# Two layers with expert blocks on one core: a bound on the experts' scatters, unmodulated rows, and one fp32 product in an output projection's last pass

## The chip, the core and the metric

The kernel runs on one core of a Trainium2 chip, in one launch. The metric is the device time in microseconds, from the start to the end of an execution. TensorE (PE in the profile) multiplies matrices and transposes, VectorE (DVE) and ScalarE (ACT) work element by element, GpSimd (POOL) does so too and issues the indirect transfers, and SyncE (SP) issues the plain ones. The granted clock of TensorE is given in the profile as a share of 2.4 GHz: 1.00 or 0.50 (1.2 GHz), and means of the two.

## The reference

T = 512 rows of width D = 1024 in fp32 go through two layers. Both have the same ending: a mixing part (attention and others) whose output is multiplied by `w_out` and added to x behind a gate, a norm, a modulation by the scale and shift of the layer's condition, and a mixture of experts on the modulated rows.

```python
mix = jnp.concatenate([attn, hg], axis=-1) @ w_out[l]
x = x + ga1 * rmsnorm(mix, ln1_post[l])
h = rmsnorm(x, ln2_pre[l]) * (1.0 + sc2) + sh2
y = hierarchical_moe(h, ...)          # layer 1: 32 experts, 2 per row
...
x = x + g_mix * (merged @ w_out)
h2 = modulate(rms_norm(x, norm_ffn_g), sh_ffn, sc_ffn).reshape(b * s, d)
y = moe_ffn(h2, ...)                  # layer 2: 64 experts, 8 per row, and a shared one
```

An expert multiplies its rows by gate and up weights (1024 x 256 each), takes silu(gate) * up, and multiplies by down weights (256 x 1024). The result, times the row's weight, is added to the row's sum over its experts. So layer 1 adds 512 x 2 = 1024 rows and layer 2 adds 512 x 8 = 4096.

## The kernel before

All instructions go through a recording helper, so each has line 131 in the profile; one has to go by the names of tiles. `whole` (line 1733) calls the stages: `dense1`, the experts of layer 1 (`e1.run`), `dense2` with `out2`, the experts of layer 2 (`e2.run`), and `last`. Within a stage, tasks are generators, and a scheduler (`Flow`, line 152) runs the one that is due first by a virtual clock, which books an estimated cost for every instruction (`Clock.note`). The order of instructions on each engine is fixed when the program is built; a change in the number of instructions may shift a few of them.

**Weights.** SP loads weights in chunks of 128 x 1024 fp32 (512 KB) into pools `w` and `wx`, in the order in which they are used, as buffers come free. In the dense stages a product of fp32 accuracy is made of three fp32r instructions (`mm3`): weights and activations are both split into `hi` (a rounded copy, by ScalarE in `split_hi`) and `lo` (the rest, by VectorE in `split_lo`). Chunks whose split isn't wanted have `raw` set; the experts multiply in plain fp32 from the raw chunk.

**Output projection of layer 1.** `dense1` runs `w_out` in two passes, p = 0 for row tiles 0 and 1, p = 1 for tiles 2 and 3 (a tile is 128 rows), each with its own eight chunks `q_["o", p]`. The activations of tile n are two halves of 128 x 512, which `mixed` (line 1036) splits. Each pass has 8 chunks x 2 tiles x 2 column halves = 32 products of 128 x 512.

**After the projection.** `Post.pair` (line 1814) takes the sums of two tiles: it adds x behind the gate, makes the norm (tiles `u`, in the code `ms`), and starts `Route.tile` (line 1903) on each. That one transposes the normed rows on TensorE, modulates the transposed copy while it leaves PSUM (VectorE and ScalarE, scale and shift per partition), and runs the router's products and the choice of experts, many small VectorE instructions. Once both tiles of the pair have been transposed (`seen`), `pair` lets GpSimd modulate the rows themselves, in place, and store them to `h2_d` (`ha_d` in layer 1, `hb_d` in layer 2). For this the gate, shift and scale are loaded as broadcast rows. `Route.choose` and `Route.finish` come after all four tiles; the experts' loads of weights wait for the numbers they give.

**Experts.** Each expert has blocks of a fixed number of slots, 16 to 128, written out in `PLAN1` (1440 slots in 32 blocks) and `PLAN2` (5296 slots in 71 blocks). `Experts.block` turns the router's result into a list of row numbers, one per slot. An empty slot p of a block gets T + p, from `beyond`. GpSimd gathers the rows of `h2_d` into `xg` by this list, with the bound T - 1, so numbers above it are skipped. `Experts.xT` (line 2244) transposes the block on TensorE, four pieces into each of two PSUM banks; ScalarE copies one bank into `xT`, VectorE the other, with one instruction each. Then come the products with gate and up weights, `a`, its transposes `aT`, the products with down weights, and `add` (line 2330): the result `y` goes to `acc_d` by an accumulating scatter of GpSimd, without a bound. `acc_d` has T + 128 rows, so that empty slots add to the last 128, which nobody reads. `zeros` clears it beforehand. The transposes of the next expert's blocks come in TensorE's order ahead of the second half of the current one's gate and up products (`run`, line 2373).

Of the kernel before, what the change touches and what calls it, by code (L numbers as in the profile page):

```python
# [12 lines left out]
BF16 = mybir.dt.bfloat16  # L13
# [3 lines left out]
ALU = mybir.AluOpType  # L17
# [4 lines left out]
P = 128  # L22
# [191 lines left out]
class Body:  # L214
# [182 lines left out]
    def steps(self, queued, n, jobs, evac, kd=KD, pre=None, early=None):  # L397
# [6 lines left out]
        def one(c, j, sel):  # L404
            ahead = None
            for i in sel:
                kind, c0, width, act, view = jobs[i]
                if outs[i] is None:
                    outs[i] = view(self.bank())
                for jj in range(c.kd):  # L410
                    s = slice(jj * n + c0, jj * n + c0 + width)
                    wt = (c.hl[0][:, s], c.hl[1][:, s])
                    ac = act(j + jj)
                    L, R = (wt, ac) if kind == "T" else (ac, wt)
                    self.mm3(outs[i], L, R, j + jj == 0, j + jj == kd - 1)
                    if jj < c.kd - 1:
                        yield
                if j + c.kd == kd:
                    evac(i, outs[i])
                if ahead:  # L420
                    self.split_lo(ahead)
                    ahead = None
                elif self.si < self.ci + self.ls and self.loaded(READY):
                    ahead = self.split_hi()
                yield
            self.split_lo(ahead)

# [103 lines left out]
    def ada_mask(self):  # L531

        nc = self.nc
        m = self.mask = self.c_const([P, 256])
# [34 lines left out]
    def ada_row(self, acc, b, part, dst, gain=None, plus=0.0, cols_=None):  # L569
# [11 lines left out]
        nc.sync.dma_start(cols(dst), r)  # L581
# [90 lines left out]
    def dense1(self, x1_d, h2_d, route, x1, acc1, acc2):  # L672
# [9 lines left out]
        for p in range(2):  # L682
            q_["o", p] = self.add_chunks(I["w_out"], D, KD)
        x1.queue(route)
# [28 lines left out]
        post = Post(self, True, mod[0:3], I["x"], x1_d, h2_d, route)  # L713
        route.mod = self.c_tile([P, 8]), self.c_tile([P, 8])
# [3 lines left out]
        def row(i):  # L718
            yield 8.0
            post.load(i, self.u)  # L720

        def ada(parts):
            for part in parts:
# [3 lines left out]
                if part < 5:  # L727
                    rows.append(fl.start(row(part - 2)))

        def zeros():  # L730
# [9 lines left out]
            for t in range(NT + 1):  # L740
                nc.sync.dma_start(acc1[t * P : (t + 1) * P], z)
                yield 5.0
            nc.sync.dma_start(acc2[T : T + P], z)
# [83 lines left out]
        for p in range(2):  # L827
            fl.until_(lambda: E.done[2 * p] and E.done[2 * p + 1] and E.att[2 * p] and E.att[2 * p + 1])
            jobs = []
            for t in (2 * p, 2 * p + 1):  # L830
                act = (lambda t: lambda j: tuple(x[:, j % 4 * P : j % 4 * P + P] for x in E.half[t][j // 4]))(t)
                jobs += [("tok", half * 512, 512, act, full) for half in range(2)]
# [203 lines left out]
    def mixed(self, E, n, half, x, done):  # L1036

        hl = self.h(F32R), self.h(F32R)
# [143 lines left out]
    def dense2(self, acc_d, x2_d, route):  # L1182
# [15 lines left out]
        route.mod = self.c_tile([P, 8]), self.c_tile([P, 8])  # L1198
# [255 lines left out]
    def out2(self, mg, t_mg, x2_d, x3_d, h2_d, route, acc_d, e2):  # L1454
# [4 lines left out]
        post = Post(self, False, m[2:5], x2_d, x3_d, h2_d, route)  # L1459
        for i in range(3):  # L1460
            post.load(i, self.r4)
# [271 lines left out]
    def whole(self):  # L1733
        nc, tc, I, fl = self.nc, self.tc, self.I, self.flow
        dr = lambda n, r=T: self.dr.tile([r, D], F32, name=n)
        x1, x2, x3, ha, hb, acc1, acc2 = dr("x1_d"), dr("x2_d"), dr("x3_d"), dr("ha_d"), dr("hb_d"), dr("acc1_d", T + P), dr("acc2_d", T + P)
# [58 lines left out]
class Post:  # L1795


    def __init__(self, body, post, rows, x_d, x1_d, h2_d, route):
        self.b, self.post, self.rows, self.x_d, self.x1_d, self.h2_d = body, post, rows, x_d, x1_d, h2_d
        self.v, self.xs = [None] * 3, {}  # L1800
        self.seen, self.evac = route.seen, [False] * 2

    def load(self, i, vec):
        self.v[i] = vec()
        self.b.bcast(self.v[i], self.rows[i])
# [8 lines left out]
    def pair(self, p, outs, then):  # L1814
        b, nc = self.b, self.b.nc
        gate, shift, scale = self.v
# [24 lines left out]
        for i in range(2):  # L1841
            if i:
                nc.scalar.activation(ms[i], xs[i], AF.Copy, scale=r[:, i : i + 1])
            else:
                nc.vector.tensor_scalar(out=ms[i], in0=xs[i], scalar1=r[:, i : i + 1], scalar2=None, op0=ALU.mult)
            ts.append(b.flow.start(then(2 * p + i, ms[i]), MARGIN2))
        yield 1
        yield from b.wait_(lambda: self.seen >= {2 * p, 2 * p + 1})
        for i in range(2):
            nc.gpsimd.tensor_tensor(out=ms[i], in0=ms[i], in1=scale, op=ALU.mult)  # L1850
            nc.gpsimd.tensor_tensor(out=ms[i], in0=ms[i], in1=shift, op=ALU.add)
            nc.gpsimd.dma_start(self.h2_d[(2 * p + i) * P : (2 * p + i + 1) * P], ms[i])
# [3 lines left out]
class Route:  # L1856
# [6 lines left out]
    def __init__(self, body, E, plan, first, chosen, router, name):  # L1863
# [6 lines left out]
        self.sels, self.parts, self.chosen, self.seen = [], [None] * NT, False, set()  # L1870
# [32 lines left out]
    def tile(self, t, h, keep=None):  # L1903
# [7 lines left out]
        self.seen.add(t)  # L1911
# [245 lines left out]
class Experts:  # L2157
# [86 lines left out]
    def xT(self, x):  # L2244
        b, C = self.b, x.C
        x.xT = self.xTs[x.n % len(self.xTs)]
        for half in range(2):
# [82 lines left out]
    def add(self, x):  # L2330
        b, nc, k = self.b, self.b.nc, 0
        y = self.mp.tile([P, D], F32, name="y", tag="y", bufs=3)[: x.C]
        for py, (n, C, g) in zip(x.py, self.parts(x.C)):
            h = 1024 // len(py) // g
            for i, o in enumerate(py):
                for q in range(g):
# [7 lines left out]
                    else:  # L2344
# [4 lines left out]
                                     compute_op=ALU.add)  # L2349
# [247 lines left out]
```

## Time and profile before

| | us |
|---|---|
| median of three runs | 2090.17 |
| lowest, highest | 2090.0, 2093.3 |
| the profiled execution | 2091.46 |
| its span, first to last instruction | 2089.7 |

| engine | busy us | share of the span |
|---|---|---|
| TensorE, products | 1807.8 | 87% |
| VectorE | 1061.4 | 51% |
| ScalarE | 559.3 | 27% |
| GpSimd | 359.7 | 17% |

| stretch, us | stage |
|---|---|
| 0 to 407 | dense work of layer 1, from about 300 on its output projection's end and the routing |
| 407 to 714 | experts of layer 1 |
| 714 to 1405 | dense work of layer 2, from about 1290 on output projection, routing, shared expert |
| 1405 to 2060 | experts of layer 2 |
| 2060 to 2090 | the last sum and norm |

The mean granted clock is 0.925. The DMA engines moved 551.8 MB. Shares of the whole span mix stages of different kinds, so they are read stage by stage, and in the routings instruction by instruction. A timeline row gives start and duration of an instruction, or of several equal ones in a row (x4), and in brackets how long its engine was idle before and what ended the idle time.

### The profile page before, as it was taken

The page shows a single profiled execution, that of the slowest core. Times are in us where ns is not written, and L with a number is a line of the kernel's source. Part 1 is how long each engine was busy: PE and PEld are TensorE (multiplying, and loading weights), DVE is VectorE, ACT ScalarE, POOL GpSimd, SP SyncE. Part 2 cuts the span into 40 slices and gives each one's busy share as a digit, 9 for nine tenths or more (in the row PEclk, how much of TensorE's full clock was granted, in tenths as well). Part 3 has the DMA queues.
Part 4 walks back from the last instruction along what each step waited for, and adds up shares of the span by engine and source line. Part 5 has one row for each costly group of instructions (what it writes and reads, how often), then busy time and mean ns, then how long its engine had stood idle before and what let it go on. Part 6 is the DMA issues. An engine that isn't in the chain of part 4 may idle for free. (4 is left out here: it accounts for less than half of the span.)

```text
span 2089.7 us, 35845 instructions
## 1 busy us (share of the span) xinstructions
PE 1807.8 (87%) x13085; PEld 1175.0 (56%) x13085; DVE 1061.4 (51%) x2885; ACT 559.3 (27%) x1146; POOL 359.7 (17%) x375
## 2 busy tenths in 40 slices
PE   4999986398878579888889998779999999999993
PEld 3777765354444457667767776655544445455551
DVE  5554766533223264466655655854544444444443
ACT  3522443211111252356653223410100000001011
POOL 1000002323222100000000211413222222222221
PEclk9999987599975689999999999989999999999997
DMA  9746323399999865776423557449999999999996
GB/s 338 267 153 231 141 80 140 138 347 364 376 381 380 340 221 184 259 234 173 146 84 111 181 188 265 172 152 361 362 359 358 348 363 367 353 360 346 357 357 227
DMA packets 180167, 551.81 MB, mean 264 GB/s; under 512 B 28290, under 2 KB 40706, under 8 KB 179988
## 3 DMA queue, kind: packets, MB, share of 16 engines
q1 hardware_dynamic: 159268, 491.10, 64.1%
q0 software_dynamic: 18560, 54.88, 10.6%
q10 hardware_dynamic: 2160, 3.50, 0.5%
q8 instruction: 105, 1.72, 0.3%
q14 instruction: 74, 0.61, 0.1%
HBM read 495.48 MB, written 60.53 MB: 266 GB/s over the span
## 5 line engine op out<-in xcount | busy, mean ns | idle before, releaser
L131 PE MATMUL bank<-w,xT 128*32 128x128 f32 (+5 forms) x2988 | 312.5, 363 | 12.4 <-DMA w<-in_w_gu 11.0
L131 PE MATMUL bank<-u,hi 128*128 128x512 f32 x800 | 262.9, 411 | 9.0 <-DVE u L131 5.6
L131 POOL DMA_INDIRECT acc_d<-y,iv x103 | 148.4, 1441 | 498.6 <-DVE y L131 156.9
L131 PEld LDWEIGHTS bank<-w,xT 128*32 128x32 f32 (+5 forms) x2988 | 148.7, 128 | 130.5 <-issue 70.9
L131 PE MATMUL bank<-wx,xT 128*32 128x128 f32 (+4 forms) x1812 | 185.5, 363 | 14.7 <-DMA wx<-in_w_gu 8.8
L131 DVE TENSOR_TENSOR y<-bank,gate 32x256 f32<-32x256 f32 (+5 forms) x228 | 128.0, 561 | 109.1 <-PE bank L131 107.2
L131 PEld LDWEIGHTS bank<-u,hi 128*128 128x128 f32 x800 | 148.6, 195 | 43.6 <-DVE u L131 7.1
L131 PE MATMUL bank<-u,lo 128*128 128x512 f32 x400 | 161.6, 404 | 10.2 <-DVE lo L131 10.2
L131 ACT ACTIVATE xT<-bank 128x128 f32<-128x128 f32 (+6 forms) x103 | 40.0, 388 | 450.1 <-PE bank L131 426.8
L131 DVE TENSOR_TENSOR lo<-w,hi 128x1024 fp32r<-128x1024 f32 x105 | 135.9, 1299 | 42.9 <-ACT hi L131 39.5
L131 PE MATMUL bank<-hi,u 128*128 128x512 f32 (+1 forms) x512 | 154.5, 386 | 1.4 <-DVE u L131 1.4
L131 PEld LDWEIGHTS bank<-ident,xg 48*128 48x128 f32 (+6 forms) x824 | 99.0, 200 | 75.6 <-issue 60.3
L131 PE MATMUL bank<-w,aT 128*32 128x256 f32 (+5 forms) x664 | 126.6, 535 | 14.6 <-DMA w<-in_w_dn 10.2
L131 PEld LDWEIGHTS bank<-wx,xT 128*32 128x32 f32 (+4 forms) x1812 | 89.8, 129 | 78.9 <-issue 38.7
L131 PE MATMUL bank<-wx,aT 128*32 128x256 f32 (+5 forms) x600 | 118.9, 524 | 6.6 <-DMA wx<-in_w_dn 6.0
L131 ACT ACTIVATE hi<-w 128x1024 fp32r<-128x1024 f32 x105 | 108.8, 1049 | 48.5 <-PE bank L131 24.4
L131 PE MATMUL bank<-ident,xg 48*128 48x48 f32 (+6 forms) x824 | 112.0, 280 | 11.0 <-DMA xg<-ha_d,iv 9.5
L131 PE MATMUL bank<-lo,u 128*128 128x512 f32 (+1 forms) x256 | 105.4, 412 | 17.1 <-DVE lo L131 16.1
L131 POOL TENSOR_TENSOR u<-u,t 128x1024 f32<-128x1024 f32 x16 | 40.3, 2518 | 427.3 <-DVE u L131 352.6
L131 DVE SCALAR_TENSOR_TENSOR a<-a,iv,bank 64x256 f32<-64x256 f32 (+3 forms) x80 | 38.5, 481 | 144.1 <-ACT a L131 144.1
L131 PEld LDWEIGHTS bank<-hi,u 128*128 128x128 f32 x512 | 97.6, 196 | 19.0 <-DVE u L131 1.8
L131 ACT ACTIVATE a<-bank 64x256 f32<-64x256 f32 (+4 forms) x129 | 43.4, 337 | 238.8 <-PE bank L131 230.5
(235 smaller groups left out, 2663.5 us busy)
## 6 DMA issues: line engine op xcount, KB each, us to landing
w<-in_w_gu SPq DMA_DIRECT2D x235, 512.0 KB, 13.4
wx<-in_w_gu SPq DMA_DIRECT2D x149, 512.0 KB, 12.5
w<-in_w_dn SPq DMA_DIRECT2D x101, 512.0 KB, 13.1
wa<-in_w_ada SPq DMA_DIRECT2D x96, 512.0 KB, 6.5
wx<-in_w_dn SPq DMA_DIRECT2D x91, 512.0 KB, 13.0
w<-in_w_in SPq DMA_DIRECT2D x68, 512.0 KB, 5.6
w<-in_w_out SPq DMA_DIRECT2D x21, 512.0 KB, 7.7
nab<-in_nab SPq DMA_DIRECT2D x48, 128.0 KB, 3.9
```

Source lines behind the costliest of these rows:

```text
L131: r = f(*a, **k)
```

## The change

It has four parts. The experts' scatters get the bound that the gathers have, so that empty slots are skipped, and `acc1_d` and `acc2_d` lose their 128 spare rows with the two stores that cleared them. `pair` stores the normed rows unmodulated, straight after the norm, without waiting for `seen`; GpSimd's sixteen multiplications and additions go, and of the three broadcast rows only the gate is loaded. The experts modulate instead, in `xT`: one copy of four pieces becomes four instructions with a scale `A` and shift `B` per partition, on ScalarE and on VectorE. The chunks of the last pass of layer 1's output projection are raw, and the activations of tiles 2 and 3 are not split, so that each of its 32 products is one fp32 instruction. The mask of `ada_mask` becomes bf16, which is a matter of space.

```diff
@@ project
                 for jj in range(c.kd):
                     s = slice(jj * n + c0, jj * n + c0 + width)
-                    wt = (c.hl[0][:, s], c.hl[1][:, s])
                     ac = act(j + jj)
-                    L, R = (wt, ac) if kind == "T" else (ac, wt)
-                    self.mm3(outs[i], L, R, j + jj == 0, j + jj == kd - 1)
+                    if c.raw:
+                        self.nc.tensor.matmul(outs[i], ac, c.w[:, s], start=(j + jj == 0), stop=(j + jj == kd - 1))
+                    else:
+                        wt = (c.hl[0][:, s], c.hl[1][:, s])
+                        L, R = (wt, ac) if kind == "T" else (ac, wt)
+                        self.mm3(outs[i], L, R, j + jj == 0, j + jj == kd - 1)
...
             self.split_lo(ahead)
+            if c.raw:
+                self.used(c)
@@ dense1
             q_["o", p] = self.add_chunks(I["w_out"], D, KD)
+        for c in q_["o", 1]:
+            c.raw = True
...
-            for t in range(NT + 1):
+            for t in range(NT):
                 nc.sync.dma_start(acc1[t * P : (t + 1) * P], z)
                 yield 5.0
-            nc.sync.dma_start(acc2[T : T + P], z)
@@ mixed
+        if n >= 2:
+            E.half[n][half] = x
+            done[n] = True
+            return
         hl = self.h(F32R), self.h(F32R)
@@ out2
-        post = Post(self, False, m[2:5], x2_d, x3_d, h2_d, route)
-        for i in range(3):
-            post.load(i, self.r4)
+        post = Post(self, False, m[2], x2_d, x3_d, h2_d, route)
+        post.load(self.r4)
@@ Post.pair
                 nc.vector.tensor_scalar(out=ms[i], in0=xs[i], scalar1=r[:, i : i + 1], scalar2=None, op0=ALU.mult)
+            nc.gpsimd.dma_start(self.h2_d[(2 * p + i) * P : (2 * p + i + 1) * P], ms[i])
             ts.append(b.flow.start(then(2 * p + i, ms[i]), MARGIN2))
-        yield 1
-        yield from b.wait_(lambda: self.seen >= {2 * p, 2 * p + 1})
-        for i in range(2):
-            nc.gpsimd.tensor_tensor(out=ms[i], in0=ms[i], in1=scale, op=ALU.mult)
-            nc.gpsimd.tensor_tensor(out=ms[i], in0=ms[i], in1=shift, op=ALU.add)
-            nc.gpsimd.dma_start(self.h2_d[(2 * p + i) * P : (2 * p + i + 1) * P], ms[i])
         yield from b.wait(*ts)
@@ Experts.xT
-            sl = slice(half * 4, half * 4 + 4)
-            if half:
-                b.nc.vector.tensor_copy(x.xT[:, sl, :C], pt[:, :, :C])
-            else:
-                b.nc.scalar.activation(x.xT[:, sl, :C], pt[:, :, :C], AF.Copy)
+            for k in range(4):
+                j = half * 4 + k
+                if half:
+                    b.nc.vector.tensor_scalar(out=x.xT[:, j, :C], in0=pt[:, k, :C], scalar1=A[:, j : j + 1], scalar2=B[:, j : j + 1], op0=ALU.mult, op1=ALU.add)
+                else:
+                    b.nc.scalar.activation(x.xT[:, j, :C], pt[:, k, :C], AF.Identity, scale=A[:, j : j + 1], bias=B[:, j : j + 1])
@@ Experts.add
         nc.gpsimd.indirect_dma_start(out=self.acc_d, out_offset=bass.IndirectOffsetOnAxis(ap=x.idx, axis=0), in_=y, in_offset=None,
-                                     compute_op=ALU.add)
+                                     bounds_check=T - 1, oob_is_err=False, compute_op=ALU.add)
```

On TensorE, at the start of the last pass of layer 1's output projection, before the change (`ident,u` are the transposes of `Route.tile`, `c_467,h` the router's products, `lo,h` and `hi,h` the pass):

```order
L131 MATMUL bank<-ident,ctx 128x128 x4
L131 MATMUL bank<-ident,u 128x128 x16
L131 MATMUL bank<-ident,h 128x128 x4
L131 MATMUL bank<-ident,ctx 128x128 x2
L131 MATMUL bank<-c_467,h 128x36 x16
L131 MATMUL bank<-ident,ctx 128x128 x2
L131 MATMUL bank<-lo,h 128x512
L131 MATMUL bank<-hi,h 128x512 x2
```

and with it:

```order
L131 MATMUL bank<-ident,ctx 128x128 x4
L131 MATMUL bank<-ident,u 128x128 x16
L131 MATMUL bank<-ident,h 128x128 x4
L131 MATMUL bank<-ident,ctx 128x128 x2
L131 MATMUL bank<-w,h 128x512
L131 MATMUL bank<-c_467,h 128x36 x16
L131 MATMUL bank<-ident,ctx 128x128 x2
L131 MATMUL bank<-w,h 128x512 x3
```

One product of the pass has moved ahead of the router's products of tiles 0 and 1; the rest follow in the same place, one instruction where there were three.

On GpSimd, at the end of layer 2's routing, before the change (three more such groups of two tensor-tensors and a store stand ahead):

```order
L131 TENSOR_TENSOR u<-u,t_11837 128x1024
L131 TENSOR_TENSOR u<-u,t_11835 128x1024
L131 DMA hb_d<-u 128x1024
L131 MEMSET xg 128x1024 x3
L131 DMA xg<-hb_d,iv 64x1024 x3
L131 MEMSET a_12888 64x128
```

and with it:

```order
L131 IOTA s 128x4
L131 CAST R<-s 128x256
L131 DMA hb_d<-u 128x1024 x4
L131 MEMSET xg 128x1024 x3
L131 DMA xg<-hb_d,iv 64x1024 x3
L131 MEMSET a_13010 64x128
```

The four stores stand together, and nothing of GpSimd's own work is left between them and the clearing of the gathers' buffers.

On ScalarE, among the experts of layer 2, before the change (`k_6764` and `k_6763` below are the scale and the shift):

```order
L131 ACTIVATE xT_12884<-bank 128x4x96
L131 ACTIVATE a<-bank 64x256
L131 ACTIVATE xT_12882<-bank 128x512
L131 ACTIVATE a<-bank 128x256
L131 ACTIVATE a<-bank 64x256
L131 ACTIVATE a_12890<-bank 64x128
L131 ACTIVATE xT_12883<-bank 128x4x96
```

and with it:

```order
L131 ACTIVATE xT_13006<-bank,k_6764,k_6763 128x96 x4
L131 ACTIVATE a<-bank 64x256
L131 ACTIVATE xT_13004<-bank,k_6764,k_6763 128x128 x4
L131 ACTIVATE a<-bank 128x256
L131 ACTIVATE a<-bank 64x256
L131 ACTIVATE a_13012<-bank 64x128
L131 ACTIVATE xT_13005<-bank,k_6764,k_6763 128x96 x4
```

The places are the same; each evacuation is four instructions long, ahead of the evacuation of `a` that follows it.

## Rows read from the trace of the kernel before

**Rows 1.** Windows: stretch and length, each engine's busy time, PEclk, DMA share, GB/s
```profile
407.00:714.00 307.00, 243.51 (x2207) 127.54 (x2203) 93.79 (x362) 46.41 (x115) 77.85 (x73) 0.81 1.02 369
1405.00:2060.00 655.00, 638.01 (x5273) 325.16 (x5269) 302.10 (x919) 62.00 (x167) 176.44 (x206) 1.00 1.03 356
```

**Rows 2.** Timeline (start, us, engine, operation): routing of layer 1, second pair
```profile
389.76 4.82 POOL L131 TENSOR_TENSOR u<-u 128x1024 f32<-128x1024 f32 x2
385.51 6.88 PE L131 MATMUL bank<-c,h 128*128 128x36 f32 x32
389.91 2.24 DVE L131 TENSOR_SCALAR s<-c,s 128x4 f32<-128x4 f32 x1
392.30 2.31 DVE L131 TENSOR_SCALAR s<-s 128x4 f32<-128x4 f32 x1
395.98 0.18 DVE L131 TENSOR_TENSOR h<-bank,c 128x36 f32<-128x36 f32 x1
396.87 0.23 DVE L131 TENSOR_SCALAR s<-c,s 128x4 f32<-128x4 f32 x1
```

**Rows 3.** Timeline of the projection's last pass; a row by form; a window
```profile
357.29 0.39 PE L131 MATMUL bank<-lo,h 128*128 128x512 f32 x1
357.98 0.40 PE L131 MATMUL bank<-lo,h 128*128 128x512 f32 x1
...
L131 PE MATMUL bank<-w,xT 128*112 128x512 f32 x48 | 23.0, 609 | 0.0
...
343.60 0.79 PE L131 MATMUL bank<-lo,h 128*128 128x512 f32 x1 [5.29 <-DVE lo L131]
308.65 0.69 DVE L131 TENSOR_TENSOR h<-h 128x512 fp32r<-128x512 f32 x1 [0.69 <-ACT h L131]
...
336.00:338.00 2.00, 2.00 (x6) 1.30 (x4) 1.46 (x10) 0.95 (x4) 0.59 (x1) 0.50 0.36 145
```

**Rows 4.** DMA queues (packets, MB, share): the whole span, then 1450 to 2050
```profile
q0 software_dynamic: 18560, 54.88, 10.6%
...
q1 hardware_dynamic: 49431, 179.06, 78.2%
q0 software_dynamic: 11496, 34.69, 24.5%
```

**Rows 5.** Waits (us in total, times, longest): 440 to 700, then 1420 to 2060
```profile
PE bank L131 <- DMA w<-in_w_gu: 10.2, 19, 1.3
...
PEld bank L131 <- DMA w<-in_w_gu: 5.0, 14, 1.1
```

**Rows 6.** Timeline: routing of layer 2
```profile
1313.43 5.15 POOL L131 TENSOR_TENSOR u<-u,t 128x1024 f32<-128x1024 f32 x2
1311.52 8.21 DVE L131 TENSOR_TENSOR u<-h,u 128x512 fp32r<-128x512 f32 x4 [1.30 <-ACT u L131]
1350.10 8.55 DVE L131 TENSOR_TENSOR u<-h,u 128x512 fp32r<-128x512 f32 x4
1388.13 0.69 DVE L131 TENSOR_TENSOR h<-h 128x512 f32<-128x512 f32 x1 [1.45 <-DMA h<-x_d]
1322.65 0.79 PE L131 MATMUL bank<-lo,u 128*128 128x512 f32 x1 [7.87 <-DVE lo L131]
1359.68 0.42 PE L131 MATMUL bank<-ident,h 128*64 128x128 f32 x1 [2.54 <-DVE h L131]
```

**Rows 7.** By tile (ns min/median/max) and timeline: evacuations, and a product on `xT`
```profile
L131 ACT ACTIVATE xT<-bank x64: 277/383/598, 1464.5 to 2047.8; 128x192 f32<-128x192 f32 x13, 128x256 f32<-128x256 f32 x11, 128x128 f32<-128x128 f32 x11, 128x320 f32<-128x320 f32 x10
...
323.99 1.50 ACT L131 ACTIVATE h<-bank,c,c 128x128 f32<-128x128 f32 x4 [0.76 <-PE bank L131]
384.05 1.37 DVE L131 TENSOR_SCALAR h<-bank,c,c 128x128 f32<-128x128 f32 x4 [2.13 <-PE bank L131]
...
1711.32 1.14 PE L131 MATMUL bank<-ident,xg 112*128 112x112 f32 x8
1720.41 1.97 PE L131 MATMUL bank<-w,xT 128*112 128x512 f32 x4
```

More of the change, by code (lines that the diff above doesn't have):

```diff
@@ L533, in ada_mask @@
         nc = self.nc
-        m = self.mask = self.c_const([P, 256])
+        m = self.mask = self.c_const([P, 256], BF16)
         nc.gpsimd.memset(m, 1.0)
@@ L580, in ada_row @@
             nc.vector.scalar_tensor_tensor(out=r, in0=r, scalar=plus, in1=gc, op0=ALU.add, op1=ALU.mult)
-        nc.sync.dma_start(cols(dst), r)
+        if cols_ is None:
+            nc.sync.dma_start(cols(dst), r)
     def norm_scale(self, x, ss, out=None):
@@ L711, in dense1, with row @@
         fl.start(bounds())
-        post = Post(self, True, mod[0:3], I["x"], x1_d, h2_d, route)
-        route.mod = self.c_tile([P, 8]), self.c_tile([P, 8])
+        post = Post(self, True, mod[0], I["x"], x1_d, h2_d, route)
+        route.mod = self.c_const([P, 8]), self.c_const([P, 8])
         rows = []
-        def row(i):
+        def row():
             yield 8.0
-            post.load(i, self.u)
+            post.load(self.u)
         def ada(parts):
@@ L726, in ada @@
                 yield from self.ada_row(acc, I["b_ada"], part, mod[part - 2], *gain, cols_={3: route.mod[1], 4: route.mod[0]}.get(part))
-                if part < 5:
-                    rows.append(fl.start(row(part - 2)))
+                if part == 2:
+                    rows.append(fl.start(row()))
         def zeros():
@@ L830, in dense1 @@
             for t in (2 * p, 2 * p + 1):
-                act = (lambda t: lambda j: tuple(x[:, j % 4 * P : j % 4 * P + P] for x in E.half[t][j // 4]))(t)
+                cut = lambda x, j: x[:, j % 4 * P : j % 4 * P + P]
+                act = (lambda t: lambda j: cut(E.half[t][j // 4], j) if p else tuple(cut(x, j) for x in E.half[t][j // 4]))(t)
                 jobs += [("tok", half * 512, 512, act, full) for half in range(2)]
@@ L1196, in ada @@
                                         cols_={3: route.mod[1], 4: route.mod[0]}.get(part))
-        route.mod = self.c_tile([P, 8]), self.c_tile([P, 8])
+        route.mod = self.c_const([P, 8]), self.c_const([P, 8])
         E = SimpleNamespace()
@@ L1735, in whole @@
         dr = lambda n, r=T: self.dr.tile([r, D], F32, name=n)
-        x1, x2, x3, ha, hb, acc1, acc2 = dr("x1_d"), dr("x2_d"), dr("x3_d"), dr("ha_d"), dr("hb_d"), dr("acc1_d", T + P), dr("acc2_d", T + P)
+        x1, x2, x3, ha, hb, acc1, acc2 = dr("x1_d"), dr("x2_d"), dr("x3_d"), dr("ha_d"), dr("hb_d"), dr("acc1_d"), dr("acc2_d")
         e1 = Experts(self, I["w_gu1"], I["w_dn1"], ha, acc1)
@@ L1795, with __init__, load @@
 class Post:
[L1798 to L1805, printed above, removed]
+    def __init__(self, body, post, gate, x_d, x1_d, h2_d, route):
+        self.b, self.post, self.gate, self.x_d, self.x1_d, self.h2_d = body, post, gate, x_d, x1_d, h2_d
+        self.v, self.xs = None, {}
+        self.evac = [False] * 2
+    def load(self, vec):
+        self.v = vec()
+        self.b.bcast(self.v, self.gate)
     def rows_of(self, p):
@@ L1815, in pair @@
         b, nc = self.b, self.b.nc
-        gate, shift, scale = self.v
+        gate = self.v
         xs, ms = self.xs.pop(p), [b.u() for _ in range(2)]
@@ L1869, in __init__ @@
         self.cnt, self.orow = b.c_const([P, E]), b.c_const([P, E])
-        self.sels, self.parts, self.chosen, self.seen = [], [None] * NT, False, set()
+        self.sels, self.parts, self.chosen = [], [None] * NT, False
     def setup(self):
@@ L1910, in tile @@
                 nc.tensor.transpose(pts[half][:, j * P : (j + 1) * P], h[:, half * 4 + j :: KD], b.ident)
-        self.seen.add(t)
         yield W
@@ L2244, in xT @@
     def xT(self, x):
-        b, C = self.b, x.C
+        b, C, (A, B) = self.b, x.C, self.route.mod
         x.xT = self.xTs[x.n % len(self.xTs)]
```

## The prediction

> **What bounds the kernel now.** I read the busy time by stage first, then who waits for whom in each stage, then single instructions where a stage was idle. Two stages of experts hold nearly half the span. In the first (407 to 714) the DMA engines are full while TensorE is busy 243.5 of 307 us at a mean clock of 0.81; in the second (1405 to 2060) TensorE is busy 638 of 655 us at clock 1.00 and the DMA engines are full too [rows 1]. So a byte less is worth its time in the first, and little in the second. Between the dense layers and the experts lie two routings, chains of small VectorE instructions in which TensorE idles; there the reader should look at VectorE instructions that take ten times their usual time while GpSimd multiplies [rows 2, 6].
>
> **Routing of layer 1: GpSimd's modulation goes.** GpSimd's tensor-tensor pairs on 128x1024 take 4.82 us; beside them one VectorE tensor-scalar on 128x4 took 2.24 us and the next 2.31, where the same instruction for the next tile took 0.23 [rows 2]. That is 2.0 + 2.1 = 4.1 us in the chain that ends in the choice of experts. Not all of it comes back: TensorE's router products run from 385.51 for 6.88 us, to 392.39, and tile 3's choice, which begins at 395.98 [rows 2], can't start before them. Without the 4.1 us tile 2's choice would end at 391.9, so tile 3 starts about 392.6: **-3.4 us**; 0 if ScalarE's exponentials turn out late, -4.1 at most. The row stores come earlier; nothing waits for them before the gathers, which need the choice. GpSimd's queue holds nothing else there that anyone waits for.
>
> **The last pass of the first output projection.** 32 products change from three fp32r instructions to one fp32 one. Three took 357.98 - 357.29 = 0.69 us at full clock; an fp32 product with 512 columns, as the experts run it, costs 23.0/24 = 0.96 us (three of the 112-row blocks, eight products each, two records a product) [rows 3]. So +0.27 x 32 = +8.6 us. Gone are the weight splits and with them the wait of 5.29 us for VectorE's `lo` [rows 3]. Gone too are the activation splits: 0.69 us on VectorE behind 0.69 us of waiting for ScalarE [rows 3], twice between 308 and 314 in the queue that leads to pair 0's norm, so the pass starts 2.8 us earlier. Net 8.6 - 5.3 - 2.8 = **+0.5 us**. Bounds: at 336 to 338 the clock was 0.50 [rows 3], and some eight products ran at half speed; should the pass without its hole be at full clock, 8 x 0.6 = 5 us come back (-4.5); if eight still run at half (8 x 0.27 = 2.2 more) and no earlier start follows, +5. The weight chunks are freed earlier or at the same time; what SP loads behind them waits for the experts' choice anyway.
>
> **Scatters of the empty slots.** Layer 1 has 1440 slots for 512 x 2 = 1024 rows, layer 2 has 5296 for 512 x 8 = 4096: 416 and 1200 empties, 4 KB each. GpSimd's queue moved 54.88 MB in all [rows 4]; 5120 gathered rows, 6736 scattered ones and twelve plain 0.5 MB stores make 54.85, so the gathers, which have the bound already, move no empty rows, and the bound should do the same for scatters. Price: between 1450 and 2050 the weights' queue took 78.2% of 600 us for 179.06 MB, 2.62 us per MB, and GpSimd's queue 24.5%, 147 us, for 34.69 MB [rows 4]. Split 4096 to 5296 that is 15.13 MB gathered, 39.6 us at the weights' price, which leaves 107.4 us for 19.56 MB scattered: 5.5 us per MB, 0.0225 us per row. Layer 1 saves 416 x 0.0225 = 9.4 us of the DMA engines' time, layer 2 1200 x 0.0225 = 27 us; at the weights' price only 4.5 and 13.
>
> In layer 1 TensorE waits 10.2 us for gate and up weights of the first pool alone [rows 5], more than the 9 us to be had: **-9 us** (-4.5 to -9.4). In layer 2 the longest such wait is 5.0 us in all, of the weight loads on gate and up weights [rows 5]. The saving can return those and no more, and 27 us is more than the lead of 11 us that a shorter routing takes from the loads: **-3.5 us**, 0 to -8. The stores of zeros that go lie in a stage bound by TensorE: 0.
>
> **Routing of layer 2.** Here GpSimd's pairs take 5.15 us, and four VectorE tensor-tensors from 1311.52 took 8.21 us, four from 1350.10 took 8.55, where one takes 0.69 [rows 6]: 4 x 0.69 = 2.8, so 5.4 and 5.8 us are standstill. TensorE's waits end behind them: 7.87 us after the first, 2.54 us after the second [rows 6]. Nothing else fills them, since the products of the pass are queued behind. I take 11.2 us of stall as **-11 us**; -6 if products ahead in TensorE's order or ScalarE's chain are next late, -13.5 with the half-clock stretches behind those waits. The gate row's two missing companions (shift, scale) save 1 MB of loads each layer, covered.
>
> **Evacuation in the experts.** Per block, one ScalarE and one VectorE copy become four and four, with scale and bias. The copy's median is 0.383 us on ScalarE [rows 7], at 64 columns. The same form as the new one, 128x128 with two columns of scalars, took 1.50 us for four on ScalarE and 1.37 on VectorE [rows 7]. For half the columns I take 15 to 20% off, an estimate: 1.28 and 1.10, so +0.9 and +0.7 us per block, 64 and 48 us over layer 2's 71 blocks. ScalarE is busy 62 of 655 us there, VectorE 302 [rows 1]. What covers it: the transposes of a block at 1711.32 have their product only at 1720.41 [rows 7], so the evacuation has some 8 us to run in. The evacuations of the tile `a`, which stand behind it in the same queues, may be pushed back a little: **+2 us**, 0 to +6.
>
> The Trainium skill ("Perfetto Trace Analysis", Optimizing Scalar/DVE Operations) speaks against this edit: each such instruction carries a fixed overhead of about 51 ns on ScalarE and 125 on VectorE when PSUM is read, so larger ones are better where the engine is saturated. By its figures three more of each are an estimated 0.15 + 0.38 = 0.53 us per block against my 0.9 and 0.7; with either the sum stays, as neither engine is saturated.
>
> **Sum.** -3.4 + 0.5 - 9 - 3.5 - 11 + 2 = -24.4 us. The profiled execution took 2091.46 us (span 2089.7 and 1.76 around it), 1.3 above the median; 2090.2 - 24.4 = **2066 us**. The ends added with no luck or all luck would be near 2088 and 2049; they are independent, so most of the forecast lies within 2052 to 2078.
>
> **Rivals.**
> *The evacuation lands on TensorE's path.* If the last of a block's `xT`, or the evacuation of `a` queued behind it, delays TensorE, each block pays up to 0.9 us: 64 - 26.4 = +37, **2128 us**. It breaks even at 26.4/71 = 0.37 us per block. For it: TensorE has next to no idle to hide anything in. Against: the 8 us of slack and the idle ScalarE. 7 in 100.
> *The transfers bind layer 2.* Then all 27 us count, 23.5 more than I take: **2042 us**. For it: DMA share 1.03 throughout [rows 1]. Against: no wait of TensorE on transfers there is longer in all than 5.0 us [rows 5]. The Trainium skill ("Perfetto Trace Analysis", Identifying the Most-Contended Engine) says that matmul busy share doesn't tell how near TensorE is to its limit and has HBM use judge the transfers; by that rule this rival would be the forecast. The trace's waits speak for TensorE. 6 in 100.
> *The bound skips the write but not its time.* Scatters keep their cost, the experts gain nothing: +12.5 on the forecast, **2078 us**. Against: the gathers' bytes. 5 in 100.
> *The fp32 pass stays at half clock.* 32 products at 1.92 us are 61 us, against 24 x 0.69 + 8 x 1.38 = 28 now: 61 - 28 - 5.3 - 2.8 = +25, so 24 more than forecast, **2090 us**. Against: at 357 this pass already ran at full speed [rows 3]. 4 in 100.
>
> **How the numbers follow.** The forecast has 78 in 100. The range 2046 to 2080 holds it but for about 4, and the third rival; left out are the first, second and fourth, 17 in 100. Measurements of this kernel tell about 0.2% (4 us) from no change. Slower by more comes from the first rival, 7 in 100; within 0.2% from the fourth and bits of the others, 5; faster the rest, 88.
>
> **What would show it.** Right: no VectorE instruction of several us in the two routings; TensorE's 7.87 us wait down to about 2; the fp32 pass without a hole; GpSimd's queue at 48.3 MB; DMA share in layer 2 below 1.0 with TensorE's busy time there unchanged. Wrong: the queue's bytes unchanged (third rival), new waits of TensorE for `xT` or `a` (first), layer 2 shorter by over 15 us (second), clock 0.50 in the pass (fourth).

## The result, and the profile after

The changed kernel takes 2075.24 us (median of four runs, 2072.05 to 2076.31) against 2090.09 us: 14.9 us less by the medians, and a ratio of 0.9911 with a 95% interval of 0.9891 to 0.9931, which is 14 to 23 us less. Measured twice more, on chips on which the kernel before takes 2097 and 2098 us, the ratio was 0.987 (0.985 to 0.9891) and 0.988 (0.9859 to 0.99), some 26 us less. The predicted 2066 us was low by 9, the range of 2046 to 2080 holds the time, and the direction was right. But that the sum came out near was in part luck: the scatters of layer 1, a term of 9 us, were worth 1.5, and the way to the second pair's transposes in layer 1, forecast at +0.5, came out 6 us shorter.

The stages tell it. Each is measured from one TensorE or GpSimd instruction to the next that both kernels have: the first transposes of each pair of rows (`ident,u`), the first of gathered rows (`ident,xg`), the last scatter of a layer, the first product on `xT`. Two profiles of the kernel before and three of the changed one:

| stage | before | before | changed | changed | changed | forecast |
|---|---|---|---|---|---|---|
| start to routing 1, first pair | 322.8 | 320.2 | 316.3 | 314.9 | 315.0 | -2.8 |
| last pass of the projection, to the second pair | 59.2 | 59.0 | 58.7 | 59.0 | 60.4 | +3.3 |
| choice, lists, first gather | 37.2 | 35.9 | 31.1 | 31.7 | 33.4 | -3.4 |
| experts of layer 1 | 294.6 | 294.4 | 292.8 | 293.3 | 292.9 | -9 |
| dense work of layer 2 | 592.5 | 597.5 | 599.5 | 598.2 | 595.1 | 0 |
| routing 2, first pair to second | 39.1 | 40.4 | 33.3 | 32.6 | 32.6 | -11, with the next row |
| routing 2, second pair to the first product | 58.5 | 57.1 | 50.2 | 50.5 | 50.6 | |
| experts of layer 2 | 660.3 | 662.8 | 663.2 | 663.9 | 662.8 | -1.5 |
| end | 25.4 | 25.4 | 25.2 | 25.1 | 25.3 | 0 |
| span | 2089.7 | 2092.6 | 2070.3 | 2069.1 | 2068.1 | -24.4 |

The profile page of the changed kernel answers [rows 4] in its line of GpSimd's queue (packets, MB, share of the span):

```profile
q0 software_dynamic: 18560, 48.28, 9.2%
```

The bytes fell by 6.6 MB, as 1616 rows of 4 KB should. The packets did not fall: 18560 before and after. A skipped row still leaves a packet; in the trace the 1616 are of 8 bytes.

The windows of its two stages of experts (length; busy time of TensorE, weight loads, VectorE, ScalarE, GpSimd; clock; DMA share; GB/s) answer [rows 1]:

```profile
394.00:701.00 307.00, 238.55 (x2210) 126.53 (x2209) 115.66 (x460) 75.76 (x211) 78.74 (x73) 0.82 1.01 364
1383.00:2045.00 662.00, 638.98 (x5281) 324.46 (x5277) 351.03 (x1134) 123.69 (x377) 178.04 (x206) 0.99 1.00 345
```

TensorE's work in layer 2 is what it was, 639 us, and the stage is as long as before, though the DMA share fell from 1.03 to 1.00. VectorE and ScalarE do 49 and 62 us more.

In routing 1 the timeline of the changed kernel answers [rows 2]:

```profile
375.21 1.05 POOL L131 DMA_DIRECT2D ha_d<-u  x2 [25.75 <-DVE u L131]
378.50 4.00 PE L131 MATMUL bank<-c,h 128*128 128x36 f32 x32
381.65 0.23 DVE L131 TENSOR_SCALAR s<-c,s 128x4 f32<-128x4 f32 x1
382.02 0.16 DVE L131 TENSOR_SCALAR s<-s 128x4 f32<-128x4 f32 x1
383.56 0.19 DVE L131 TENSOR_TENSOR h<-bank,c 128x36 f32<-128x36 f32 x1
```

GpSimd only stores. The two VectorE instructions that took 2.24 and 2.31 us take 0.23 and 0.16. The router's products take 4.00 us instead of 6.88, and the next tile's choice follows them at 383.56, 5.1 us after those products began; before it was 10.5.

Before the change, each of the two stalls ended where one of GpSimd's instructions did: VectorE's at 392.15 and 394.61, GpSimd's at 392.11 and 394.58. They aren't tied to a kind of instruction either. In the second profile of the kernel before, where the two tensor-scalars took 0.23 and 0.16 us, a tensor-tensor on 32 columns and a conversion of two stood instead, again up to the ends of GpSimd's pair at 389.15 and 391.57:

```profile
386.80 4.77 POOL L131 TENSOR_TENSOR u<-u 128x1024 f32<-128x1024 f32 x2
386.39 2.82 DVE L131 TENSOR_TENSOR h<-h,s 128x32 f32<-128x32 f32 x1
389.77 1.82 DVE L131 CAST s<-s 128x2 f32<-128x2 uint32 x1
```

The pass with fp32 products, as in [rows 3]:

```profile
316.33 3.65 PE L131 MATMUL bank<-ident,u 128*128 128x128 f32 x16 [12.92 <-DVE u L131]
323.45 1.10 PE L131 MATMUL bank<-w,h 128*128 128x512 f32 x2 [2.19 <-issue]
331.34 4.48 PE L131 MATMUL bank<-w,h 128*128 128x512 f32 x6
344.75 17.43 PE L131 MATMUL bank<-w,h 128*128 128x512 f32 x40
375.06 3.65 PE L131 MATMUL bank<-ident,u 128*128 128x128 f32 x16 [12.87 <-DVE u L131]
```

The transposes that open it come at 316.33 instead of 322.82. No hole is left for a `lo`; a product is two records, so 17.43 us for 40 records are 0.87 us each (forecast 0.96), at a granted clock of 1.00 from 345 to 362, and the three at 331.34 took 1.5 us each, where the clock was still low (0.60 in the mean of 331 to 335.8).

Routing 2, as in [rows 6]:

```profile
1298.61 1.16 POOL L131 DMA_DIRECT2D hb_d<-u  x2 [36.00 <-DVE u L131]
1303.37 2.49 DVE L131 TENSOR_TENSOR u<-h,u 128x512 fp32r<-128x512 f32 x4
1309.42 0.48 PE L131 MATMUL bank<-lo,u 128*128 128x512 f32 x1
1336.57 1.29 DVE L131 TENSOR_TENSOR u<-h,u 128x512 fp32r<-128x512 f32 x2
1342.57 0.30 PE L131 MATMUL bank<-ident,h 128*64 128x128 f32 x1 [0.39 <-DVE h L131]
```

Four tensor-tensors take 2.49 us where they took 8.21. The fourth `lo` product behind the router's, for which TensorE waited 7.87 us, now follows without a wait (1309.42), and the wait of 2.54 us is down to 0.39.

### The profile page after: what moved, and what is told of

The parts are those of the page before. It is cut to its first block, busy times and chain, and to the rows that moved or that the text cites. A ratio compares the mean times of both kernels' runs of the same rounds, so it can differ in the third digit from the quotient of the medians.

```text
span 2070.3 us, 36447 instructions
## 1 busy us (share of the span) xinstructions
PE 1802.5 (87%) x13053; PEld 1162.9 (56%) x13053; DVE 1096.6 (53%) x3182; ACT 640.6 (31%) x1443; POOL 322.4 (16%) x359
## 3 DMA queue, kind: packets, MB, share of 16 engines
q0 software_dynamic: 18560, 48.28, 9.2%
## 5 line engine op out<-in xcount | busy, mean ns | idle before, releaser
L131 ACT ACTIVATE xT<-bank,k,k 128x32 f32<-128x32 f32 (+6 forms) x412 | 132.5, 405 | 447.7 <-PE bank L131 402.6
L131 DVE TENSOR_TENSOR lo<-w,hi 128x1024 fp32r<-128x1024 f32 x97 | 124.2, 1286 | 39.6 <-ACT hi L131 39.4
L131 DVE TENSOR_SCALAR xT<-bank,k,k 128x32 f32<-128x32 f32 (+6 forms) x412 | 113.3, 339 | 18.2 <-PE bank L131 14.7
L131 ACT ACTIVATE hi<-w 128x1024 fp32r<-128x1024 f32 x97 | 100.5, 1049 | 34.0 <-PE bank L131 15.4
L131 POOL DMA_INDIRECT xg<-hb_d,iv x71 | 71.1, 1001 | 169.8 <-PE bank L131 70.2
L131 PEld LDWEIGHTS bank<-u,lo 128*128 128x128 f32 x400 | 77.5, 194 | 32.7 <-DVE lo L131 15.6
```

Source lines behind the costliest of these rows:

```text
L131: r = f(*a, **k)
```

## Experiments

**The kernel before again, and the changed one again.** No edit.

> The kernel before once more, to have its stages from the same chip as the next runs. The dense work of layer 2, from the last scatter of layer 1 to the first transposes of layer 2's routing, took 592.5 us in the first profile of this kernel, 599.5 in that of the changed one, and 597 to 603.5 in four kernels that change nothing there. If the changed kernel loses 6 us there, this run shows 592 to 594 again; if it is the first profile that was short, 597 to 603.

The dense work of layer 2 took 597.5 us in this profile. Thirteen profiles, none of which changes TensorE's work in that stage, range from 592.5 to 607.2 there. So the 7 us that the first pair of profiles seems to lose is the spread of that stage, which is read in no comparison below; what makes it vary was not found.

> The changed kernel once more, with an interval. The parts measured alone gave -0.23% (bound), -1.0% (rows) and -0.05% (fp32 pass) against the kernel before. If they add up, 0.987 of the time before, 26 us shorter; if parts take gains from each other (the pass and the rows both shorten the same stretch of VectorE's queue), 0.990 to 0.991, 18 to 21 us. Experts of layer 1, from the first transposes of gathered rows to the last scatter: 292 to 293 us against 294 to 295 without the bound.

Ratio 0.987 (0.985 to 0.9891). The parts alone, below, give -0.23, -1.0 and -0.05%, in sum -1.28: within the intervals they add up and take little from each other.

**The bound alone.**

```diff
...
-                             compute_op=ALU.add)
+                             bounds_check=T - 1, oob_is_err=False, compute_op=ALU.add)
```

> The kernel before with only the bound on the experts' scatters. Theory of the prediction (a skipped row gives back 0.0225 us of the DMA engines' time where they are full): the experts of layer 1 9 us shorter, those of layer 2 3.5 us, 2077 to 2078 us. Rival (the first stage is bound by bytes per second, not by the share of time that packets hold the DMA engines: 1.7 MB at 0.37 MB per us are 4.6 us at most, and the trace of the changed kernel shows this stage only 2.3 us shorter): 2 to 5 us in layer 1, 0 to 3 in layer 2, 2083 to 2088 us. GpSimd's queue should move 48.3 MB with both.

Ratio 0.9977 (0.9963 to 0.999), 2 to 8 us. In its profile the experts of layer 1 take 294.0 us, against 294.4 and 294.6, and those of layer 2 663.7, against 660.3 and 662.8: the first is shorter by half a microsecond, not by 9. In the changed kernel, whose evacuations stand in the same queues, the bound is worth 1.7 us in the first (294.7 to 293.0 beside the rows-only kernel below) and 2.5 in the second (665.8 to 663.3). One profile doesn't show where the rest of its 5 us lies. The prediction's price is refuted, and the rival's 4.6 us isn't seen either.

**Pricing a scattered row.** The changed kernel with the bound at row 256:

```diff
-                             bounds_check=T - 1, oob_is_err=False, compute_op=ALU.add)
+                             bounds_check=T // 2 - 1, oob_is_err=False, compute_op=ALU.add)
```

> The changed kernel with the bound at half of the rows, so that the scatters leave out the experts' sums of rows 256 to 511 as well: about 512 scattered rows less in layer 1 and 2048 in layer 2, 2.1 and 8.4 MB. This prices a scattered row where the transfers bind. Theory of the prediction (0.0225 us of full DMA engines per row): experts of layer 1 11.5 us shorter than in the changed kernel, 281 us. Rival (bytes at 0.37 MB per us): 5.7 us, 287 us. Second rival (the weights' stream sets the stage and the scatters run beside it): 0 to 3 us, 290 to 293. Layer 2: 0 to 2 us with all, if TensorE bounds it; 40 us if the transfers do.

Since the sums of the upper rows are left out, layer 2 routes other data and does a block more at its end; the total (0.9987 of the kernel before) says nothing, and only layer 1 is read. Its experts took 292.9 us, with the changed kernel at 292.8 to 293.3. Half of the filled rows gone, nothing won.

**No scatters in layer 1 at all** (`gate` is None for the experts of layer 1 only; the rest of the kernel is the changed one).

```diff
         x.py = None
+        if self.gate is None:
+            return
...
```

> The changed kernel without any scatter in the experts of layer 1: their sums aren't added, this part is left out, and what layer 2 routes by it is other data, so only the stage of layer 1's experts is read. With half of the rows skipped its length was 292.9 us as in the changed kernel (292.8, 293.3), although GpSimd's queue fell from 11.3% to 8.0% of the DMA engines' time. If the weights' stream sets this stage by itself (about 0.343 MB per us whatever runs beside it), 291 to 294 us again. If what counts is the number of packets, which skipped rows don't lower, or the whole of the scatters' time, 10% of 293: 265 to 285 us.

From the first transposes of gathered rows to the last down products, in this kernel and in the changed one:

```profile
407.00 1.11 PE L131 MATMUL bank<-ident,xg 64*128 64x64 f32 x8 [9.76 <-DMA xg<-ha_d,iv]
665.49 1.75 PE L131 MATMUL bank<-w,aT 128*32 128x256 f32 x16 [0.29 <-DVE aT L131]
```
```profile
405.57 1.11 PE L131 MATMUL bank<-ident,xg 64*128 64x64 f32 x8 [9.73 <-DMA xg<-ha_d,iv]
684.77 1.93 PE L131 MATMUL bank<-w,aT 128*32 128x256 f32 x16 [0.28 <-DVE aT L131]
```

258.5 us against 279.2 (between all the other profiles this stretch differs by 3 us): the scatters do cost this stage 20.7 us, but skipping their rows gives nearly none of it back. (By the same two instructions the kernel before takes 279.9 and the half-bound one 278.8.) The DMA view of 440 to 680 shows what differs: the kernel before in its second profile, the changed one, the half-bound one, and the one without scatters; for each the weights' queue q1 and GpSimd's queue q0, in packets, MB and share:

```profile
DMA packets 25501, 89.38 MB, mean 372 GB/s; under 512 B 3695, under 2 KB 3742, under 8 KB 25477
q1 hardware_dynamic: 22244, 80.67, 87.7%
q0 software_dynamic: 3233, 8.39, 14.8%
```
```profile
DMA packets 25654, 89.04 MB, mean 371 GB/s; under 512 B 3978, under 2 KB 3978, under 8 KB 25627
q1 hardware_dynamic: 22519, 82.00, 89.9%
q0 software_dynamic: 3108, 6.69, 11.6%
```
```profile
DMA packets 25697, 87.26 MB, mean 364 GB/s; under 512 B 4456, under 2 KB 4456, under 8 KB 25670
q1 hardware_dynamic: 22509, 81.96, 91.8%
q0 software_dynamic: 3161, 4.95, 8.2%
```
```profile
DMA packets 25981, 92.55 MB, mean 386 GB/s; under 512 B 3446, under 2 KB 3446, under 8 KB 25955
q1 hardware_dynamic: 24491, 89.17, 97.5%
q0 software_dynamic: 1464, 3.04, 4.3%
```

From the first to the third, q0's bytes fall by 41% and its share from 14.8 to 8.2%, while its packets stay: they become packets under 512 bytes, 3695, 3978, 4456 in both queues together. The weights' queue carries 80.67, 82.00 and 81.96 MB in the same 240 us. Only in the fourth, with q0's packets halved, does it carry 89.17. The four windows lie at slightly different places of the stage. Read over the 200 us that begin 25 us behind its first transposes, the weights' queue carries 66.20, 66.47, 67.17 and 72.98 MB, beside 2848 packets of q0 three times and 1456 in the fourth.

Most of the time that q0 gave up was taken. In these 200 us the weights' queue holds the engines for 86.7, 88.4 and 91.1% of the time, but with 4.4 points more it moves 1.5% more: its 4 KB packets took longer, 170, 173 and 177 ns in the mean (172 in the fourth). What makes them longer was not found.

Each of the three steps takes about as many bytes off q0 in the views above, 1.70, 1.74 and 1.91 MB, and only the last shortens the stage by more than 1 us. So what the weights' stream pays for is not in proportion to the bytes of the scatters. Nor is it the time for which the packets of skipped rows hold an engine, 10 ns each in the trace. Whether it is the number of packets, or something else that comes with a scatter and goes only with it (its reading of the sums before it adds, the instruction itself), or a limit that only the last step gets below, these runs don't separate. A bound that skips every row and keeps the scatters would help to; no run here has it.

The Trainium skill ("DMA: Bandwidth & Descriptors", Why small descriptors are slow) names a fixed cost per descriptor beside its bytes, a few cycles and 32 bytes. No run here shows that this cost is at work: 1440 scattered slots less gave 20.7 us, 416 empty ones made small some 1.5. By the Trainium skill's 32 bytes, 1440 slots are 46 KB, an estimated 0.14 us at the weights' 332 GB/s, so that part of it is far too small.

**The rows alone.** Only `Post.pair`, the row loads and `Experts.xT` as in the change; the scatters have no bound, the pass is split as before. (The mask in bf16 and the stores of scale and shift rows that nobody reads any more go with this part, too.)

> The kernel before with only the unmodulated rows: GpSimd modulates nothing, the experts' evacuations of xT do. Theory of the prediction: routing of layer 1 3.4 us shorter, that of layer 2 11 us, evacuations 2 us longer, 2078 us. What the trace of the changed kernel suggests: routing of layer 2 14 us shorter, experts of layer 2 3 us longer, 2073 to 2077 us. Rival: the 6 us that the changed kernel loses in the dense work of layer 2 come from this part (the longer life of its two columns, or the order of work), then 2080 to 2083 us and the dense work of layer 2 is 598 us long instead of 592.

Ratio 0.99 (0.9883 to 0.9917), 17 to 25 us: this part is four fifths of the change. Against the second profile of the kernel before: pass 55.8 us for 59.0, choice 32.3 for 35.9, routing 2 84.3 for 97.5, experts of layer 2 665.8 for 662.8. The 5.29 us of [rows 3] have become

```profile
338.68 0.80 PE L131 MATMUL bank<-lo,h 128*128 128x512 f32 x1 [3.90 <-DVE lo L131]
```

as this pass still splits its weights: GpSimd's first pair of modulations had made that `lo` later, too, by 1.4 us. With them went a wait of 0.91 us for an activation's `lo`, and the wait for the second pair's norm, the last of the pass, fell from 14.15 to 12.89. The dense work of layer 2 took 596.9 us here, so the rival that puts a loss there falls.

**GpSimd's modulations left out.**

```diff
-            nc.gpsimd.tensor_tensor(out=ms[i], in0=ms[i], in1=scale, op=ALU.mult)
-            nc.gpsimd.tensor_tensor(out=ms[i], in0=ms[i], in1=shift, op=ALU.add)
```

> The kernel before without GpSimd's multiplications and additions in the two routings, so that the rows that go to the experts aren't modulated: this part of the computation is left out. Nothing else changes, so it prices GpSimd's work beside VectorE alone. Prediction: 3.4 us in the routing of layer 1 and 11 in that of layer 2, 14.4 us, 0.993 of the time before. What the rows-only kernel suggests, which also pays 4 to 5 us for its evacuations: 4 us or more in the first, 14 in the second, 1 to 3 us more from products that run at clock 1.00, 0.988 to 0.990. If it is not GpSimd's work that holds VectorE up, 0 to 2 us.

Here too layer 2 routes other data and does a block more, so its total (1.004) isn't read. Up to the first product of layer 2's experts nothing else differs from the kernel before: pass 54.2 us for 59.0, choice 33.3 for 35.9 (58.9 to 60.5 and 35.9 to 37.2 in the four profiles with GpSimd's work and the split pass), routing 2 32.8 + 50.5 = 83.3 for 97.5. That is 7.4 us in layer 1 and 14.2 in layer 2 from taking eight plus eight GpSimd instructions away, and the changed kernel has the same 83.1 to 83.5 us in routing 2. In place of the 8.21 and 7.87 us of [rows 6] this trace has

```profile
1300.39 2.50 DVE L131 TENSOR_TENSOR u<-h,u 128x512 fp32r<-128x512 f32 x4 [1.32 <-ACT u L131]
1306.50 0.50 PE L131 MATMUL bank<-lo,u 128*128 128x512 f32 x1 [2.88 <-DVE lo L131]
```

GpSimd's work was what held VectorE.

**The fp32 pass alone.** Only the raw chunks, the unsplit halves and the branch in `project`.

> The kernel before with only the raw chunks and unsplit activations in the last pass of layer 1's output projection. Theory of the prediction: +0.5 us, 2090 to 2091 us. Rival, from the trace of the changed kernel (the first pair's norm comes 6.5 us earlier because two splits, their waits and two evacuations leave VectorE's queue, and the pass itself takes no longer): second pair's transposes 7 us earlier, 2082 to 2084 us; if the router's products after them also run at clock 1.00 instead of 0.50, up to 3 us more, 2079 to 2081.

Ratio 0.9995 (0.9982 to 1.0009): no change that can be told. In the profile the first pair's transposes come at 315.6 instead of 320.2 (-4.6), the pass takes 61.1 us instead of 59.0, the choice 36.4 instead of 35.9: 2 us are left of it when the experts begin. Single profiles differ by 3 to 4 us at that start (319.6 to 322.8 in the six with the splits, 314.5 to 318.3 in the eight without), so these 2 us are rough. In the changed kernel the pass is no longer than before, since GpSimd's part goes too.

**The evacuation alone**, as in the change, with ones and zeros for scale and shift:

```diff
-            if half:
-                b.nc.vector.tensor_copy(x.xT[:, sl, :C], pt[:, :, :C])
-            else:
-                b.nc.scalar.activation(x.xT[:, sl, :C], pt[:, :, :C], AF.Copy)
+            for k in range(4):
+                j = half * 4 + k
...
```

> The kernel before with only the evacuations of xT as four instructions with two columns of scalars on each engine, here ones and zeros, so that nothing else changes (GpSimd still modulates the rows; the mask in bf16 makes room for the columns). This is the price of the evacuation alone. Prediction: +2 us (0 to 6), 2090 to 2096. Rival one: it lands on TensorE's path, 0.9 us a block, +64 us. Rival two, from the changed kernel's trace: TensorE's waits for a grow by 3 us and its weight loads' by 8 in layer 2, +3 to +5 us, and in layer 1, bound by transfers, nothing.

Ratio 1.001 (0.9995 to 1.0025). The experts of layer 2 take 665.3 us against 660.3 and 662.8, those of layer 1 294.2 as before. TensorE's waits in layer 2 (us in total, times, longest), in the second profile of the kernel before, then here:

```profile
PE bank L131 <- DVE a L131: 10.8, 20, 1.1
```
```profile
PE bank L131 <- DVE a L131: 13.9, 25, 1.1
```

So 110 us of added engine time cost TensorE some 3 us, where an evacuation holds the tile `a` up. The first rival, +64 us, falls.

**Two other ways to share the evacuations**, from the changed kernel, to win those 3 us back: all on ScalarE, and the second bank on VectorE for every other block only.

```diff
-                if half:
+                if False:
...
-                if half:
+                if half and x.n % 2:
```

> The changed kernel again, so that the two versions below have it beside them on the same chip: 0.987 to 0.991 of the time before.

> The changed kernel with all eight evacuations of xT on ScalarE, none on VectorE. In the changed kernel TensorE waits 15.6 us in the experts of layer 2 for the tile a, whose last step is VectorE's; before the change 10.8. If it is VectorE's queue that is late (its evacuations stand ahead of that step), these waits go back to about 10 and 3 to 5 us are won: 0.998 of the changed kernel. If it is ScalarE, which makes the first step of a and would have eight instructions ahead of it, the waits grow: 5 to 15 us lost.

> The changed kernel with the second bank of xT evacuated by VectorE for every other block only, by ScalarE for the rest. Between the changed kernel and the one above in both theories: 2 us won or 2 to 7 lost.

Against the kernel before on the same chip: changed 0.988 (0.9859 to 0.99), all on ScalarE 0.9985 (0.9971 to 0.9999), every other block 0.9918 (0.9902 to 0.9933). Both lose, 22 and 8 us against the changed kernel. With all on ScalarE the experts of layer 2 take 682.7 us instead of 662.8. TensorE's waits and VectorE's longest one for ScalarE, in the changed kernel and then with all on ScalarE:

```profile
PE bank L131 <- DVE a L131: 14.0, 26, 1.1
DVE a L131 <- ACT a L131: 68.6, 53, 3.9
```
```profile
PE bank L131 <- DVE a L131: 14.1, 21, 3.8
PE bank L131 <- DVE oh L131: 11.1, 9, 1.9
DVE a L131 <- ACT a L131: 161.7, 69, 5.3
```

The waits for `a` don't shrink, and a new one appears for VectorE's next tile, `oh`: ScalarE makes the first step of `a`, now behind eight evacuations, and VectorE stands waiting for it with `oh` behind. The window of this stage shows the rest of the loss:

```profile
1390.00:2072.00 682.00, 650.93 (x5279) 327.97 (x5275) 271.34 (x853) 207.94 (x660) 178.69 (x207) 0.98 0.98 335
```

The same products keep TensorE busy for 650.9 us instead of 639, at a granted clock of 0.98 where the changed kernel has 0.99. ScalarE at 208 of 682 us busy is not short of time, only late. No version beat the changed kernel.

## Why the prediction was right, and where it was wrong

*Routing of layer 2.* The mechanism was right and mis-sized: 14.2 us, not 11 (bounds 6 to 13.5). The stalls of 5.4 and 5.8 us came back in full, and 3 us more. The trace of the kernel before shows 1.4 of them: a tensor-scalar on 64 columns took 1.62 us beside GpSimd's clearing of `xg`, and the same one for the next tile 0.25. The rest wasn't taken apart; the upper bound had allowed 2.3 for stretches at half clock.

*Routing of layer 1.* Forecast -3.4, measured -7.4 with GpSimd's work alone taken away, 4.8 of it in the pass and 2.6 in the choice. The step that failed is where I looked: only the second pair's stall was counted. The first pair's falls into the projection's last pass, where it made the `lo` for which TensorE waited 1.4 us later and drew out two more waits; I had charged those 5.29 us to the split alone. The bound by TensorE's router products held: the next tile's choice starts just behind them, at 383.56. They took 4.00 us in the changed kernel and 6.88 before, but 4.14 in the second profile of the kernel before, so the change is not what shortened them.

*The fp32 pass.* +0.5 forecast, about -2 alone and not distinguishable from nothing; within its bounds. The earlier start was 4.6 us instead of 2.8: two evacuations behind the splits in VectorE's queue moved into time in which it had waited. The products were cheaper (0.87 for 0.96 us). The fourth rival falls: the clock was 1.00 from 345 to 362.

*Scatters in layer 1.* This is the step that was wrong: -9 forecast, -4.5 as the smaller end, -0.5 to -1.7 measured. I took the share of time that packets hold the DMA engines for a capacity, and a row's part of it for what it gives back. The share did fall, by 3.2 points of 240 us for 1.7 MB, 4.5 us per MB where the working had 5.5; the stage didn't follow, as the weights' packets grew longer instead. "The bound should do the same for scatters" came true in bytes, but a packet per skipped row stays, and bytes alone had been counted. The third rival, to which I gave 5 in 100, was right in what it gave this stage, nothing, but not in its mechanism: the time of the scatters' packets did fall. That its total of 2078 us is near the first measurement is chance.

The Trainium skill ("Perfetto Trace Analysis", Identifying the Most-Contended Engine) warns of just this: with 16 DMA engines their occupancy misleads. The runs agree: GpSimd's queue went from 14.8 to 8.2% of that time and the weights came no faster.

*Scatters and evacuation in layer 2.* -3.5 and +2 forecast; the bound gave about 2.4 (665.8 to 663.3), the evacuation cost 3 to 5. Together +1.7 where -1.5 was expected; both small, both of the right sign. The first rival falls with the evacuation's price. The second, 27 us, falls too: the engines moved 345 GB/s where they had moved 356, and the stage is no shorter. TensorE bounds it. The 0.53 us per block from the Trainium skill's overheads ("Perfetto Trace Analysis", Optimizing Scalar/DVE Operations) was a third of it: the busy times rose by 62 + 49 us over 71 blocks, which is 1.6 us per block, as the rows had given.

*The sum.* By the stages' means over the profiles: -6.1 before the pass, -4.5 in the choice, -1.5 and +1.7 in the experts, -14.3 in routing 2, -22 in all with the dense work's spread of some +3, which belongs to no part. The misses of +7.5 in the experts of layer 1 and +3 in those of layer 2, of -7.4 in layer 1's pass and routing together and -3 in layer 2's routing cancelled, which is luck. (The ends of the terms add up to 2091 and 2051 us, where the prediction has 2088 and 2049.)

## What to carry to other kernels

An engine whose own work is waited for by nobody can still cost time, by holding up an engine that is waited for: look for instructions that take several times their usual time, and see whose instruction runs beside them and ends where they end. Before a transfer is priced by its share of the DMA engines, ask whether the stream that is waited for speeds up when it goes, and count packets as well as bytes: a bound that skips a row need not skip its packet. And spare time on an engine doesn't make work free there; what counts is which later instruction stands behind it in the queue.

## What the runs showed of the hardware

An indirect accumulating scatter with a bound moves no bytes for a skipped row but keeps its packet (18560 packets with 54.88 and with 48.28 MB; the packets of skipped rows have 8 bytes and hold an engine for 10 ns). Skipping 416 of 1440 rows, or some 928, left the experts of layer 1 within 2 us of 280; leaving the scatters out took 20.7 us off, and the weights' queue went from 332 to 365 GB/s (66.47 and 72.98 MB in 200 us). In the changed and the half-bound kernel the time that the scatters' packets gave up went into longer packets of the weights (170, 173, 177 ns). A VectorE tensor-scalar on four columns took 2.24 us instead of 0.23 beside a GpSimd tensor-tensor on 128x1024, and ended where that one ended; so it is not only the wide instructions with two inputs that stand still.
